# The second unit of differential attention ends ten groups of products later, and its results get rooms of their own

## The chip, the cores and the metric

One NeuronCore of a Trainium2 chip runs the whole program. The metric is device time in microseconds (us), the median of several runs. Engines are named as the profile names them: PE (matrix products), PEld (its weight loads), DVE (vector), ACT (activation), POOL (GpSimd), SP (which starts the DMAs here).

## The reference, cut to what matters

Two layers act on x (512 tokens x 1024, float32). Each normalises x, projects it, runs three branches side by side, gates each, and projects the sum back:

```
h = rms_norm(x, norm_g) * (1 + scale(c)) + shift(c);  proj = h @ w_in       # 3712 columns
A: 4 heads, two softmax maps each:  oa = rms_norm((softmax(q1 k1) - lam*softmax(q2 k2)) @ v) * (1 - lam_init) * silu(ga)
B: 6 heads, dilated windows (masked softmax over 512 keys):                    ob = attention(q, k, v) * silu(gb)
C: 4 heads of retention with a state carried over chunks:                      oc = rms_norm(retention) * silu(gc)
x = x + gate(c) * (concat(oa, ob, oc) @ w_out)
```

## The kernel before, in words

All large products run as three products of split operands: an operand is a high part and a rest (`whi`, `wlo` for weights, `hT`, `hL` for the activations), and `products` (L337) adds high x high, high x rest and rest x high in one PSUM bank, the tile `acc`, of which there are four. Such a set for two row blocks of the weights is a *group* of six products. The program is a list of numbered groups; `at(g, fn)` (L164) hangs a step behind group g, and `issue` walks through the list. In the first layer, groups 16 to 31 project the first unit of branch A (two of its heads; `Unit`, `Diff`), 32 to 47 the first of B, 48 to 63 the second unit of A, 64 to 79 and 80 to 95 the second and third of B, 96 to 111 the gate of branch C (its four token tiles take the four `acc` banks), 112 to 123 the gate of branch B (three blocks, three banks, lines L342 to L344), 124 to 155 the output projection. The second layer has the same order 172 groups further on. A unit's attention runs behind the projections of the units after it.

The list gives priorities, not the order of the queues: a planner in the framework places every instruction on its engine by costs and due times of its own, and hands a tile a room of its pool when one is free. So a step whose room is still held is placed later, and others go by.

The end of a unit of A is four steps. `finish` (L755) copies the attention's result from PSUM into `oat` (ACT). `finish2` (L760) turns it by four transposes on PE (`tr4`, one PSUM bank), copies that into `oao` (ACT), squares it (`oasq`, POOL), sums, and takes the power -1/2 (DVE, POOL). `finish3` scales `oao` (DVE) and multiplies by the gate `ga` (POOL). `finish4` turns it back and splits it into the two output tiles `o` that the output projection reads from group 132 on.

`oat`, `oao` and `oasq` lie in the pool `ep`, tag "e", of five rooms. In the same five lie the scores of A (`e`) and of B (`sb`, two to a row of 128 queries, from the mask step L807 until they are transposed), and `cth`, the gate of branch C: `gate_done` (L987, groups 108 to 111) computes tanh of an `acc` bank into `cth`, and a DVE step of L159 then reads the bank for the last time.

The score products use two PSUM banks (`sc`). The conditioning's gate uses them as well: `ada_steps` ends in a product into `ada_ps` (L479) and a copy into `gate` (ACT), which for the second half lies in the room of the second A unit's `ga`, and so waits for `finish3`.

For the second unit of A, `finish` is planned at 102 (48 + 54), `finish2` at 106, `finish3` at 118, `finish4` at 122:

```
            at(g + FIN2, self.finish2, g + FIN2)      # FIN2, FIN3, FIN4 = 4, 12, 16
            at(g + FIN3, self.finish3)
            at(g + FIN4, self.finish4)
```

Of the kernel before, what the change touches and what calls it, by code (L numbers as in the profile page):

```python
# [9 lines left out]
F32 = mybir.dt.float32  # L10
# [7 lines left out]
S = 512  # L18
L = 2
P = 128  # L20
# [3 lines left out]
DK_A, DV_A = 32, 64  # L24
# [22 lines left out]
SETUP, TABLES, RET_T, TAB1 = 12, 12, 19, 9        # L47
N_A1, N_B1, N_SOFT = 5, 5, 9
E_T1, E_T2, E_X, E_QF, E_SCALE_A, E_SCALE_B = 1, 1, 1, 0, 0, 0
FIN2, FIN3, FIN4 = 4, 12, 16  # L50
X_BACK = 2


# [81 lines left out]
def encoder(ctx, tc, x, c, norm_g, w_ada, b_ada, w_in, w_out, params, consts, out):  # L135
    nc = tc.nc
    pool = lambda name, bufs, **kw: ctx.enter_context(tc.tile_pool(name=name, bufs=bufs, **kw))
    one = pool("one", 1)
# [5 lines left out]
    ep = pool("ep", 5)  # L144
# [10 lines left out]
    def act(o, i, f=AF.Copy, **kw):  # L155
        A.activation(o, i, f, **kw)  # L156

    def stt(o, a, s, b, op0, op1):
        V.scalar_tensor_tensor(o, a, s, b, op0, op1)  # L159
# [4 lines left out]
    def at(g, fn, *args):  # L164
        plan.setdefault(g, []).append((fn, args))
# [118 lines left out]
    class Piece:  # L284


        def __init__(self, src, n, where=None, gains=(None, None)):
            self.src, self.n, self.where, self.gains = src, n, where, gains
# [5 lines left out]
        def split(self):  # L294
            if self.where:
                parts = self.where()
            else:
                parts = [[wp.tile([P, 2, 512], F32R, name=z)] for z in ("whi", "wlo")]
            self.hi, self.lo = ([z[:, k, :self.n] for z in y for k in range(z.shape[1])] for y in parts)
            k = 0  # L300
            for hi, lo in zip(*parts):
                m = hi.shape[1]
                r2, h2, l2 = self.raw[:, k:k + m, :self.n], hi[:, :, :self.n], lo[:, :, :self.n]
                g2 = self.gains[k:k + m]
                if not any(g is not None for g in g2):
                    act(h2, r2)

                for z, g in enumerate(g2):
                    if g is not None:
                        act(h2[:, z], r2[:, z], AF.Copy, scale=g)  # L310
                    elif any(y is not None for y in g2):
                        act(h2[:, z], r2[:, z])
                for z, g in enumerate(g2):
                    if g is None:
                        V.tensor_tensor(l2[:, z], r2[:, z], h2[:, z].bitcast(F32), OP.subtract)  # L315
                    else:
                        stt(l2[:, z], r2[:, z], g, h2[:, z].bitcast(F32), OP.mult, OP.subtract)
                k += m
# [34 lines left out]
    def tok_(t):  # L353
        return slice(t * P, (t + 1) * P)
# [72 lines left out]
    def in_chunk(l, cols, done, first=False):  # L427

        n = sum(z for _, z in cols)
        wheres = [room("stk"), None, rows((one, "b0"), (one, "b1"), (one, "b2"), (three, "v")),  # L430
                  rows((three, "v"), (three, "v"), (two, "pt"), (two, "pt"))]
        pieces = [Piece(win_src(l, k0, cols), n, wheres[k0 // 2] if first else None) for k0 in range(0, KD, 2)]
        g0 = len(groups)
        ps = {}

        def group(i, t):
            def emit():
                if t not in ps:
                    ps[t] = acc_p.tile([P, 512], F32, name="acc")
                p = pieces[i]  # L440
                products(ps[t][:, :n], [(hT[:, 2 * i + k, tok_(t)], hL[:, 2 * i + k, tok_(t)]) for k in range(2)],
                         p.hi, p.lo, n, i == 0, i == 3)
            return emit

        order = [(i, t) for t in range(NT) for i in range(4)] if first else [(i, t) for i in range(4) for t in range(NT)]
        for j, (i, t) in enumerate(order):
            groups.append(group(i, t))
            if i == 3:
                at(g0 + j, lambda t=t: done(t, ps[t], g0))
        for i, p in enumerate(pieces):  # L450
            piece_plan(p, g0 + (i if first else 4 * i))
        return g0, pieces
# [42 lines left out]
    def mod_steps(l, q):  # L495
        return ada_steps(l, [(q * 256, 256), (D + q * 256, 256)], lambda ps: mod_use(q, ps, mod_gain(l, q)))
# [72 lines left out]
    def tr4(blocks):  # L569
        ps = tr_p.tile([P, 4, P], F32, name="tr")  # L570
        for i, b in enumerate(blocks):
            T.transpose(ps[:, i, :], b, ident)  # L572
        return ps
# [12 lines left out]
    def rms_end(s, n, width):  # L586
        V.tensor_scalar(s, s, 1.0 / width, EPS, OP.mult, OP.add)  # L587
        pow_half(s, s, n)
# [130 lines left out]
                                 start=k == 0, stop=k == NT - 1)  # L719

    class Diff(Attention):
        def __init__(self, unit, g0, gap, oh, ol):
            self.oh, self.ol = oh, ol
            self.m = {}
            super().__init__(unit, g0, gap)

# [26 lines left out]
                self.e[qt, h] = self.m[2 * h]  # L753

        def finish(self, g):  # L755
            self.ob = ep.tile([P, S], F32, name="oat", tag="e")
            act(self.ob, self.pv)
            at(g + FIN2, self.finish2, g + FIN2)

        def finish2(self, g):  # L760
            ps = tr4([self.ob[:, tok_(t)] for t in range(NT)])
            o = self.o = ep.tile([P, 8, DV_A], F32, name="oao", tag="e")
            act(o.rearrange("p g d -> p (g d)"), ps.rearrange("p t m -> p (t m)"))
            sq = ep.tile([P, 8, DV_A], F32, name="oasq", tag="e")
            G.tensor_tensor(sq, o, o, OP.mult)
            ss = self.ss = sm.tile([P, 8], F32, name="oass")
            r0 = self.r0 = sm.tile([P, 8], F32, name="oar0")
            V.reciprocal(r0.rearrange("p (t h) -> p t h", h=2), self.ssum[:, :, 0::2])
            V.tensor_reduce(ss, sq, AX.X, OP.add)
            V.tensor_tensor(ss, ss, r0, OP.mult)  # L770
            V.tensor_tensor(ss, ss, r0, OP.mult)
            rms_end(ss, 8, DV_A)
            at(g + FIN3, self.finish3)
            at(g + FIN4, self.finish4)

        def finish3(self):
            o, ss = self.o, self.ss
# [5 lines left out]
        def finish4(self):  # L783
            on = self.o.rearrange("p (t h) d -> p t (h d)", h=2)
            ps = tr4([on[:, t] for t in range(NT)])
            split(self.oh, self.ol, ps.rearrange("p t m -> p (t m)"))

    class Dilated(Attention):
        def __init__(self, unit, g0, gap, ob, sg, out):
# [212 lines left out]
    def layer(l):  # L1002
# [15 lines left out]
        def out_pair(k):  # L1018
            oAB[k] = [one.tile([P, S], F32R, name=f"o{k}{z}", tag=f"s{2 * k + z}") for z in range(2)]
            return oAB[k]  # L1020

        def start_a(u, un, g, gap):
            Diff(un, g, gap, *out_pair(u))

        def start_b(u, un, g, gap):

# [4 lines left out]
        for kind, u, where, start, gap in (("A", 0, "A", START_A0, GAP_A0), ("B", 0, "B", START_B0, GAP_B0), ("A", 1, "A", START_A1, GAP_A1),  # L1031
                                           ("B", 1, "B", START_B1, GAP_B1), ("B", 2, "A", START_B2, GAP_B2)):
            if kind == "A":
                un = Unit(l, DK_A, 0, where)
                g0, _ = in_chunk(l, [(u * P + j * 256, P) for j in range(4)], un.done)
            else:
                un = Unit(l, DH_B, 2, where)
                g0, _ = in_chunk(l, [(COL_QB + u * P + j * 384, P) for j in range(3)], un.done)
# [48 lines left out]
        def plan_ada(steps, g, gap, g_end=0):  # L1087
            loads, adds, end = steps
            for i in range(4):
                at(g + gap * i - 6, loads[i])  # L1090
                at(g + gap * i, adds[i])
            at(max(g + gap * 4, g_end), end)
            return g + gap * 4
# [21 lines left out]
        for hf in range(2):  # L1115
            cols = slice(hf * 512, hf * 512 + 512)
            ps = {}
# [58 lines left out]
            for j, t in turns:  # L1176
# [9 lines left out]
                g = len(groups) - 1  # L1186
# [9 lines left out]
        if not last:  # L1196
            g = g_gb - MODS
            for q in range(4):
                g = plan_ada(mod_steps(l + 1, q), g, 3)
# [116 lines left out]
```

## Time and profile before

| | us |
|---|---|
| median of 3 runs (649.25 to 651.51) | 651.46 |
| the profiled execution, its own time | 650.6 |
| its span, first to last instruction | 648.7 |

The profile is of one execution; a row of a timeline gives start, duration, engine, line, operation and tiles, and in brackets how long the engine stood idle before it and what ended that.

### The profile page before, as it was taken

The page shows a single profiled execution, that of the slowest core. Times are in us where ns is not written, and L with a number is a line of the kernel's source. Part 1 is how long each engine was busy: PE and PEld are TensorE (multiplying, and loading weights), DVE is VectorE, ACT ScalarE, POOL GpSimd, SP SyncE. Part 2 cuts the span into 40 slices and gives each one's busy share as a digit, 9 for nine tenths or more (in the row PEclk, how much of TensorE's full clock was granted, in tenths as well). Part 3 has the DMA queues.
Part 4 walks back from the last instruction along what each step waited for, and adds up shares of the span by engine and source line. Part 5 has one row for each costly group of instructions (what it writes and reads, how often), then busy time and mean ns, then how long its engine had stood idle before and what let it go on. Part 6 is the DMA issues. An engine that isn't in the chain of part 4 may idle for free.

```text
span 648.7 us, 10469 instructions
## 1 busy us (share of the span) xinstructions
PE 622.2 (96%) x3487; PEld 512.2 (79%) x3487; DVE 491.8 (76%) x1206; ACT 344.4 (53%) x756; POOL 163.7 (25%) x183
## 2 busy tenths in 40 slices
PE   6899999999999996999999999999999999899997
PEld 1788888987888873677779998997788787677786
DVE  4787676689988987898969364768997997578443
ACT  4855263566646665564424344455756577566410
POOL 1105452514350510200411041633323340020000
PEclk9799999999999999999999999999999999999999
DMA  8998123535555556476643322235565453604211
GB/s 302 295 293 238 55 70 98 135 98 146 150 152 176 141 176 161 160 248 201 216 156 110 90 73 66 71 104 159 134 176 137 135 145 112 161 34 149 80 65 66
DMA packets 87277, 93.03 MB, mean 143 GB/s; under 512 B 7188, under 2 KB 68276, under 8 KB 87224
## 3 DMA queue, kind: packets, MB, share of 16 engines
q1 hardware_dynamic: 87224, 92.37, 48.0%
q8 instruction: 28, 0.46, 0.3%
q14 instruction: 25, 0.20, 0.1%
HBM read 72.42 MB, written 4.19 MB: 118 GB/s over the span
## 4 chain that ended last, share of the span: by engine, by line
PE 79%; DVE 9%; issue 4%; DMA 3%; POOL 3%; ACT 2%; SPq 1%; POOLq 0%; ACTq 0%
PE acc L346 16%; PE acc L348 16%; PE acc L347 16%; PE tr L572 8%; PE pv L718 5%; PE sc L741 2%; DMA x<-in_x_dram 2%; PE acc L344 1%; PE acc L342 1%; PE acc L343 1%; PE sc L802 1%; PE sc L803 1%; DVE wlo L315 1%; PE co L971 1%; DVE pt L708 1%
## 5 line engine op out<-in xcount | busy, mean ns | idle before, releaser
L346 PE MATMUL acc<-whi,hT 128*128 128x384 f32 (+1 forms) x424 | 154.7, 365 | 0.0
L347 PE MATMUL acc<-wlo,hT 128*128 128x384 f32 (+1 forms) x424 | 151.8, 358 | 0.0
L348 PE MATMUL acc<-whi,hL 128*128 128x384 f32 (+1 forms) x424 | 151.8, 358 | 0.0
L315 DVE TENSOR_TENSOR wlo<-raw,whi 128x384 fp32r<-128x384 f32 (+1 forms) x130 | 80.7, 650 | 26.7 <-ACT whi L156 26.4
L199 POOL TENSOR_TENSOR qkss<-qkss,nhalf 128x4 f32<-128x4 f32 (+1 forms) x40 | 52.6, 1315 | 128.3 <-DVE qkss L587 127.3
L346 PEld LDWEIGHTS acc<-whi,hT 128*128 128x128 f32 x424 | 80.0, 189 | 6.1
L348 PEld LDWEIGHTS acc<-whi,hL 128*128 128x128 f32 x424 | 79.8, 188 | 6.2
L347 PEld LDWEIGHTS acc<-wlo,hT 128*128 128x128 f32 x424 | 80.0, 189 | 5.5
L156 ACT ACTIVATE whi<-raw 128x768 fp32r<-128x768 f32 (+2 forms) x67 | 59.5, 890 | 39.7 <-PE acc L348 33.8
L159 DVE SCALAR_TENSOR_TENSOR ada_acc<-raw,cs,ada_acc 128x512 f32<-128x512 f32 x86 | 64.3, 749 | 3.9 <-DMA raw<-in_w_ada_dram 3.3
L156 ACT ACTIVATE e<-sc,mx 128x512 f32<-128x512 f32 x64 | 43.9, 689 | 35.5 <-DVE mx L743 16.9
L743 DVE TENSOR_REDUCE mx<-sc 128x1 f32<-128x512 f32 x64 | 43.5, 685 | 9.5 <-PE sc L741 8.8
L156 ACT ACTIVATE sb<-sb,mx 128x512 f32<-128x512 f32 x48 | 34.4, 717 | 20.4 <-DVE mx L807 20.2
L718 PE MATMUL pv<-pt,v 128*64 128x256 f32 x320 | 38.9, 385 | 1.0 <-DVE pt L708 0.9
L156 ACT ACTIVATE pt<-tr 128x512 f32<-128x512 f32 x40 | 23.8, 596 | 23.1 <-PE tr L572 22.9
L572 PE MATMUL tr<-cst,sb 128*128 128x128 f32 x192 | 30.7, 283 | 5.3 <-DVE nat L159 2.2
L807 DVE CUSTOM_DVE_ANT_0 sb<-sc,cst 128x512 f32<-128x512 f32 x48 | 32.1, 683 | 4.4 <-PE sc L803 2.6
L572 PEld LDWEIGHTS tr<-cst,sb 128*128 128x128 f32 x192 | 21.9, 142 | 16.0 <-ACT pt L156 7.7
L718 PEld LDWEIGHTS pv<-pt,v 128*64 128x64 f32 x320 | 21.2, 136 | 16.2 <-DVE pt L708 5.5
L708 DVE COPY pt<-tr 128x512 f32<-128x512 f32 x40 | 27.4, 684 | 7.8 <-PE tr L572 7.8
L639 POOL TENSOR_TENSOR qkn<-qkraw,qkss 128x256 f32<-128x256 f32 x40 | 30.0, 751 | 5.9 <-DVE qkraw L635 2.0
L741 PE MATMUL sc<-stk,stq 96*128 96x512 f32 x64 | 27.3, 434 | 1.0 <-ACT e L156 0.9
(294 smaller groups left out, 1367.8 us busy)
## 6 DMA issues: line engine op xcount, KB each, us to landing
raw<-in_w_ada_dram SPq DMA_DIRECT2D x64, 256.0 KB, 3.2
raw<-in_w_in_dram SPq DMA_DIRECT2D x48, 192.0 KB, 2.9
raw<-in_w_in_dram SPq DMA_DIRECT2D x24, 384.0 KB, 3.4
raw<-in_w_in_dram SPq DMA_DIRECT2D x32, 256.0 KB, 3.4
raw<-in_w_ada_dram SPq DMA_DIRECT2D x16, 512.0 KB, 5.1
raw<-in_w_out_dram SPq DMA_DIRECT2D x32, 256.0 KB, 3.0
x<-in_x_dram SPq DMA_DIRECT2D x8, 512.0 KB, 4.2
stB<-nat SPq DMA_DIRECT2D x32, 128.0 KB, 2.4
```

The lines of the kernel that those rows point to most:

```text
L156: A.activation(o, i, f, **kw)
L159: V.scalar_tensor_tensor(o, a, s, b, op0, op1)
L199: G.tensor_tensor(o, i, nhalf[:, :n], OP.pow)
L315: V.tensor_tensor(l2[:, z], r2[:, z], h2[:, z].bitcast(F32), OP.subtract)
L346: T.matmul(ps, ah, hi[i], start=s_, stop=False)
L347: T.matmul(ps, ah, lo[i], start=False, stop=False)
L348: T.matmul(ps, al, hi[i], start=False, stop=e_)
L572: T.transpose(ps[:, i, :], b, ident)
L708: V.tensor_copy(pt, ps)
L718: T.matmul(self.pv[h * 64:h * 64 + 64, i * 256:i * 256 + 256], self.u.v[:, k, h * 64:h * 64 + 64], self.pt[h][:, k], start=k == 0, stop=k ...
L741: T.matmul(ps, self.u.stq[0:96, m, tok_(qt)], self.u.stk[0:96, m], start=True, stop=True)
L743: V.tensor_reduce(mx, ps, AX.X, OP.max, negate=True)
```

## The change

The second unit of A gets offsets of its own: `finish2` 14 groups behind `finish` (not 4), `finish3` 6 and `finish4` 9 behind that, so 116, 122 and 125 (not 106, 118, 122). The first unit keeps 4, 12, 16. For both units `oat` and `oao` leave the pool "e": they lie in the pool `one`, in the rooms of the unit's output pair (tags s0 and s1, or s2 and s3), and the pair itself is taken in `finish4`, when `oat` and `oao` are through, rather than at the unit's start. `oasq` stays in "e". No computation is added or left out.

```diff
-FIN2, FIN3, FIN4 = 4, 12, 16
+FIN_A = (4, 12, 16), (14, 6, 9)
-        def __init__(self, unit, g0, gap, oh, ol):
-            self.oh, self.ol = oh, ol
+        def __init__(self, unit, g0, gap, fin, k, out_pair):
+            self.k, self.out_pair, self.fin = k, out_pair, fin
         def finish(self, g):
-            self.ob = ep.tile([P, S], F32, name="oat", tag="e")
+            self.ob = one.tile([P, S], F32, name="oat", tag=f"s{2 * self.k + 1}")
             act(self.ob, self.pv)
-            at(g + FIN2, self.finish2, g + FIN2)
+            at(g + self.fin[0], self.finish2, g + self.fin[0])
         def finish2(self, g):
             ps = tr4([self.ob[:, tok_(t)] for t in range(NT)])
-            o = self.o = ep.tile([P, 8, DV_A], F32, name="oao", tag="e")
+            o = self.o = one.tile([P, 8, DV_A], F32, name="oao", tag=f"s{2 * self.k}")
...
-            at(g + FIN3, self.finish3)
-            at(g + FIN4, self.finish4)
+            at(g + self.fin[1], self.finish3)
+            at(g + self.fin[2], self.finish4)
         def finish4(self):
...
-            split(self.oh, self.ol, ps.rearrange("p t m -> p (t m)"))
+            split(*self.out_pair(self.k), ps.rearrange("p t m -> p (t m)"))
         def start_a(u, un, g, gap):
-            Diff(un, g, gap, *out_pair(u))
+            Diff(un, g, gap, FIN_A[u], u, out_pair)
```

## Rows read from the trace of the kernel before

**Rows 1.** The page: busy time of the engines; PE's busy tenths in 40 slices.
```profile
PE 622.2 (96%) x3487; PEld 512.2 (79%) x3487; DVE 491.8 (76%) x1206; ACT 344.4 (53%) x756; POOL 163.7 (25%) x183
...
PE   6899999999999996999999999999999999899997
```

**Rows 2.** Windows: from:to us, length, busy by engine, then PEclk, DMA share, GB/s.
```profile
232.00:272.00 40.00, 33.81 (x190) 23.98 (x188) 34.54 (x83) 22.76 (x49) 5.29 (x5) 0.96 0.57 162
...
260.00:262.00 2.00, 2.00 (x8) 1.41 (x8) 1.75 (x6) 0.88 (x2) 0.00 (x0) 0.50 0.86 259
```

**Rows 3.** Timeline of PE, first layer, end of branch C's gate products.
```profile
241.07 0.39 PE L802 MATMUL sc<-stB,stC 128*128 128x512 f32 x1
...
241.52 0.34 PE L347 MATMUL acc<-wlo,hT 128*128 128x384 f32 x1
...
243.44 0.60 PE L572 MATMUL tr<-cst,sb 128*128 128x128 f32 x4
243.79 0.42 PE L346 MATMUL acc<-whi,hT 128*128 128x384 f32 x1
...
244.22 0.33 PE L348 MATMUL acc<-whi,hL 128*128 128x384 f32 x1
...
251.04 0.66 PE L572 MATMUL tr<-cst,sb 128*128 128x128 f32 x4 [0.69 <-ACT pt L156]
...
257.22 0.66 PE L572 MATMUL tr<-cst,oat 128*128 128x128 f32 x4 [0.78 <-DVE pt L708]
...
259.54 0.79 PE L342 MATMUL acc<-hT,whi 128*128 128x512 f32 x1
```

**Rows 4.** Windows by line (L572 twice, L802 twice, L718): PE busy (count), PEld.
```profile
244.30:259.50 15.20, 5.37 (x32) 3.37 (x32) 0.98 0.69 169
558.70:567.60 8.90, 3.28 (x20) 2.09 (x20) 1.00 0.81 198
...
244.30:259.50 15.20, 1.94 (x4) 0.76 (x4) 0.98 0.69 169
558.70:567.60 8.90, 0.95 (x2) 0.38 (x2) 1.00 0.81 198
...
244.30:259.50 15.20, 1.95 (x16) 1.06 (x16) 0.98 0.69 169
```

**Rows 5.** Timeline of ACT and DVE, first layer, around the same stretch.
```profile
239.93 0.59 ACT L156 ACTIVATE oat<-pv 128x512 f32<-128x512 f32 x1
...
244.07 0.69 DVE L807 CUSTOM_DVE_ANT_0 sb<-sc,cst 128x512 f32<-128x512 f32 x1
...
244.59 0.85 ACT L156 ACTIVATE whi<-raw 128x768 fp32r<-128x768 f32 x1
...
257.92 0.60 ACT L156 ACTIVATE oao<-tr 128x512 f32<-128x512 f32 x1 [2.19 <-PE tr L572]
258.41 0.49 ACT L156 ACTIVATE cth<-acc 128x384 f32<-128x384 f32 x1
```

**Rows 6.** Timeline of PE and ACT, second layer, the same place.
```profile
559.23 0.66 PE L572 MATMUL tr<-cst,sb 128*128 128x128 f32 x4 [0.33 <-ACT pt L156]
...
567.64 0.50 PE L342 MATMUL acc<-hT,whi 128*128 128x512 f32 x1 [0.31 <-DVE cth L159]
...
566.52 0.49 ACT L156 ACTIVATE cth<-acc 128x384 f32<-128x384 f32 x1
```

**Rows 7.** Timeline, first layer: second half of the conditioning's gate; POOL and DVE.
```profile
232.62 1.02 PE L479 MATMUL ada_ps<-ada_acc,ones 128*128 128x512 f32 x2
...
271.49 0.60 ACT L156 ACTIVATE gate<-ada_ps 128x512 f32<-128x512 f32 x1 [1.50 <-POOL oao L781]
...
272.14 0.50 PE L802 MATMUL sc<-stk,stq 128*128 128x512 f32 x1 [0.63 <-ACT gate L156]
...
258.59 1.04 POOL L765 TENSOR_TENSOR oasq<-oao 128x512 f32<-128x512 f32 x1 [24.36 <-ACT oao L156]
...
270.46 1.88 DVE L315 TENSOR_TENSOR wlo<-raw,whi 128x384 fp32r<-128x384 f32 x2
```

## The prediction

> **What bounds the kernel now.** I read the page first: PE is busy 96% of the span, DVE 76%, so the kernel is bound by PE wherever PE has work [rows 1]. A gain must therefore come from places where PE stands, and a cost must make it stand. PE's slices show where: between the first two and the last, all 37 are 9s but for the 6 at place 16 and the 8 at place 35 [rows 1]. A slice is 648.7 / 40 = 16.2 us, so they are 243 to 259 and 551 to 568, one in each layer. The windows put numbers to the first: in 232 to 272 PE is busy 33.81 of 40 us and its granted clock averages 0.96; in 260 to 262 the clock is 0.50, that is the lower level of 1.2 GHz, and what came before it was PE with holes in its work [rows 2].
>
> The timeline of PE then shows what is missing. The last product of C's gate starts at 244.22, and the first of B's gate at 259.54 [rows 3]; in the second layer the first of B's gate waits until 567.64 [rows 6]. In between PE does only attention. Weights are not what lacks: the last ones that could be split had their copy at 244.59 [rows 5]. What lacks is a PSUM bank. All four `acc` hold C's gate until `gate_done` has read them, and its first `cth` starts on ACT at 258.41, directly behind `oao` at 257.92 [rows 5], which follows the turn of `oat` at 257.22 [rows 3]. 1.13 us later the first product of B's gate starts. So `cth` waits for a room of the five of "e", and the room it gets is `oat`'s, held since 239.93 [rows 5]. That the rooms are full is seen on the other holders: an `sb` starts at 244.07 [rows 5], 0.03 us after the set of turns of an older `sb` from 243.44 ends [rows 3]. Two rows of `sb` are four rooms, `oat` is the fifth.
>
> The second layer repeats it: `cth` at 566.52, first product 1.12 us later at 567.64 [rows 6].
>
> **How much lies open.** In 244.30 to 259.50 PE has 32 transposes (8 sets), 4 score pairs and one set of 16 value products [rows 4]. At full rate a set costs 0.35 (243.44 to the product at 243.79) and a pair 0.45 (241.07 to 241.52) [rows 3]; the values took 1.95 [rows 4]. 8 x 0.35 + 4 x 0.45 + 1.95 = 6.55, so of 15.2 us 8.65 are open. In the second layer 5 sets, 2 pairs and one set of values in 8.9 us [rows 4]: 4.60, open 4.30. The low clock cost (1 - 0.96) x 40 = 1.6 us more in the first layer [rows 2].
>
> **The change, part by part.**
>
> *`oat` and `oao` out of "e", and `finish2` ten groups later.* Each request for a room then gets the release before the one it got. The last `sb` of B's second unit takes what the set before 251.04 releases, and the first `cth` what the set at 251.04 releases, at 251.04 + 0.66 = 251.70, not what `oat` leaves. `oao` and `oasq`, which asked ahead of `cth`, now ask behind it. With the same 1.13 us from `cth` to product, B's gate starts at 252.83 and not 259.54: 6.71 us to fill. In these the other work of PE is at most the values (1.95), three sets (1.05) and one pair (0.45), 3.45; `oat`'s set goes, but comes back as 0.35 in a full stretch. Regained: 6.71 - 3.45 - 0.35 = 2.9, and the clock's 1.6 if it doesn't fall: 4.5. In the second layer the set at 559.23 [rows 6] releases at 559.89, the first product is at 561.01 and not 567.64; 6.63 - 3.45 - 0.35 = 2.8. Together 7.3.
>
> The bounds. If `cth` gets a room as soon as its bank is summed, nothing is open: 8.65 + 1.6 + 4.30 - 0.70 = 13.9. If nothing moves, -0.7. DVE is a bound of its own in the first layer: busy 34.54 of 40 [rows 2], it has 5.5 us to give there unless work is put off, so I stay near the row with 4.5.
>
> *The steps moved.* `finish2` has four transposes (PE), one copy (ACT), the square and the power (POOL), a reciprocal, a sum and three small steps (DVE); none starts a DMA, so SP's queue is only touched through rooms. On POOL they pass a memset of `ada_acc`. They now lie beside B's gate, where PE has products to run; the turns I counted.
>
> The square is one price to weigh: 1.04 us, begun at 258.59 after 24 us of an idle POOL [rows 7], while DVE had little to do; moved, it runs beside a full DVE. By the Trainium skill (SBUF — State Buffer, "Who interferes with whom") a DVE instruction with two SBUF inputs is blocked for the whole of a POOL instruction that reads SBUF. The trace agrees as far as it goes: beside the POOL multiplication that ended ahead of 271.49, two `wlo` steps of 384 columns took 1.88 [rows 7], where a step of 512 columns takes 0.69 [rows 5]. By that rule DVE would lose up to 1.04 us a layer, and the gain would be up to 2.1 us less if DVE decided. I leave the sum as it is, for the bound by DVE leaves 1 us.
>
> *The second half of the conditioning's gate.* It adds no wait, but lengthens one. `ada_ps` holds one of two score banks from 232.62 until the copy at 271.49, which stood 1.50 us for POOL's multiplication by `ga` in `finish3`; PE then stood 0.63 us for the copy [rows 7]. `finish3` moves from 118 to 122. Behind the copy on ACT are the exponentials of B's third unit, and PE's score product waits for it. Below: the earlier start of B's gate makes up for the four groups, cost nothing. Above: every score row of the third unit (four a layer) runs on one bank and its second head waits for the first's mask step, 0.69 [rows 5], and its own half pair, 0.22: 0.9 x 8 = 7.2. Four groups are 24 products of half a pair, 24 x 0.225 = 5.4 us; the start is 6.7 earlier. So I take the value near the row: one such wait in each layer, where there is one in the first now: +0.6.
>
> *`finish4` at 125, not 122.* Its results are read from 132 on: seven groups, 42 products x 0.225 = 9.5 us, for a set of turns, a copy and a subtraction. Cost nothing; with that cover gone, PE would stand for these, some 0.7 us each.
>
> *The rooms s0 to s3.* Their earlier tenants, C's values, are read last at the end of C's chunks, long before 70 and 102; `finish4`'s pair takes rooms that its own turns have just released. Nothing.
>
> *The first unit.* Its `oao` held a room of "e" for 16 groups while the second unit needed four to a row. There PE's slices are 9s throughout [rows 1]; bounds 0 to -1.5 (a tenth of a slice), I take 0.
>
> Sum: 7.3 - 0.6 = 6.7. The profiled execution took 650.6 (span 648.7 and 1.9 around it): 643.9. The median is 0.86 above it, so 651.46 - 6.7 = 644.8.
>
> **Rivals.**
>
> *The gap closes wholly.* The room freed is there from 239.93 on, and C's banks are summed at 244; a `cth` that is ready then may be given it at once. For it: weights for B's gate are ready. Against: the `sb` of B's second unit are ahead in the list and ask too, and DVE's 5.5 us. 651.46 - 13.9 + 0.6 = 638.2, and with part of it 641.
>
> *The room goes elsewhere, or DVE was the limit.* The planner hands rooms by its own times; with `sb` taking every early room and DVE full, as it is until about 253, the third and fourth rows come no sooner, and `cth` still follows the last turns. Then PE gains what it loses: 648.5 to 653, say 651. Against it: two of three holders ahead of `cth` are gone.
>
> *The score bank, on the other side: slower.* If B's gate starts only a little earlier (half of the gain, 3.3) and `ga` is read late, behind the second score row of B's third unit, all eight rows pay: 651.46 - 3.3 + 7.2 = 655.4. It decides from the point where the copy into `gate` ends later than that second row. For it: 39 us of hold already [rows 7], and `finish3` later in the list. Against: while one score waits, PE has up to nine groups of B's gate to run, and a planner that fills with those pays little.
>
> **How the numbers follow.** Forecast (641 to 648.5) 0.55; closed wholly 0.15; no change 0.18; score bank 0.12. What this measurement can tell is about 0.5%, 3.3 us. All of the first two cases lie below 648.2 but for a sliver, so faster 0.70; same 0.18; slower 0.12. The range that leaves out about the bank's 0.12 above, some of the upper end of no change and the tail under the second case is 638.5 to 652; the forecast's own is 641 to 648.5.
>
> **What would show it.** Right: the first L342 product near 253 and 561 less what was gained before, in front of the turn of `oat`; no 6 and no 8 among PE's 9s; no 0.50 in the clock there; `cth` first on ACT without `oao` ahead of it. The score bank would show as PE's waits for the copy into `gate` or for a mask step of B's third unit, well over 0.63. If the first L342 product is still more than 12 us behind C's last, the room was not the cause; if it is early and the time stays, look where PE stands next, at DVE's late `wlo` and B's third unit.

## The result, and the profile after

The changed kernel takes 644.04 us (median of 4 runs, 643.31 to 644.49) beside 650.88 us for the kernel before: a ratio of 0.9897, 95% interval 0.9876 to 0.9918. The forecast was 644.8. The profiled execution took 644.29 us, its span 642.2.

The page after, the lines that answer to [rows 1], with the clock's line: engines, PE's busy tenths, PE's granted clock in tenths.

```profile
PE 620.4 (97%) x3487; PEld 512.2 (80%) x3487; DVE 492.3 (77%) x1206; ACT 343.1 (53%) x756; POOL 163.9 (26%) x183
...
PE   6899999999999997999999999999999999999997
...
PEclk9799999999999997999999999999999999999999
```

The 8 at place 35 has gone, the 6 at place 16 is only a 7, and the clock has a 7 at place 16, which it did not have before. The window of [rows 2] again, after the change:

```profile
232.00:272.00 40.00, 36.37 (x200) 26.79 (x199) 36.50 (x86) 23.86 (x51) 0.69 (x2) 0.91 0.68 197
250.00:252.00 2.00, 2.00 (x12) 1.18 (x10) 2.00 (x4) 0.49 (x1) 0.00 (x0) 0.50 0.90 204
```

PE is busy 2.56 us more of the 40, but the mean clock is 0.91, so the low clock costs up to (1 - 0.91) x 40 = 3.6 us, 2 more than before. PE's timeline of the first layer shows where it fell (compare [rows 3]); the stretch between the last product of C's gate and the first of B's is called the seam below:

```profile
241.95 0.42 PE L348 MATMUL acc<-whi,hL 128*128 128x384 f32 x1
...
246.31 0.63 PE L572 MATMUL tr<-cst,sb 128*128 128x128 f32 x4 [1.94 <-DVE nat L159]
247.63 0.71 PE L572 MATMUL tr<-cst,sb 128*128 128x128 f32 x4 [0.69 <-ACT pt L156]
249.12 3.68 PE L718 MATMUL pv<-pt,v 128*64 128x256 f32 x16 [0.78 <-DVE pt L708]
...
254.50 0.59 PE L342 MATMUL acc<-hT,whi 128*128 128x512 f32 x1
```

and ACT's, where `cth` no longer follows `oao` [rows 5]:

```profile
248.46 0.47 ACT L156 ACTIVATE cth<-acc 128x384 f32<-128x384 f32 x1
...
274.56 0.60 ACT L156 ACTIVATE oao<-tr 128x512 f32<-128x512 f32 x1 [1.77 <-PE tr L572]
...
285.10 0.60 ACT L156 ACTIVATE gate<-ada_ps 128x512 f32<-128x512 f32 x1 [2.32 <-POOL oao L782]
```

`cth` starts 0.12 us after the set of turns of 247.63 ends: by its time it got the room that this set released, as the prediction had it. A bank was free from about 249.6, but PE had the values, a set and a score pair in front of the first product, and its clock had fallen: the 16 value products took 3.68 us, not 1.95 [rows 4].

In the second layer (compare [rows 6]) nothing is left open: PE's two rows are the last product of C's gate and the first of B's.

```profile
558.72 0.33 PE L348 MATMUL acc<-whi,hL 128*128 128x384 f32 x1
558.89 0.40 PE L342 MATMUL acc<-hT,whi 128*128 128x512 f32 x1
```

Where the time went is best read as a lead: how much sooner than before the same product or turn starts in PE's timeline. Below: the first product with `whi`, at 64.99 before and ahead of every step that an edit moves ("start"); the first product into `ada_ps`, at 229.34 before and ahead of the seam ("229 us"); the first product of B's gate and of the output projection in the first layer, the first turn of the next layer's activations, the first product of the output projection in the second layer, the last product.

| us sooner than before | start | 229 us | B's gate, layer 1 | projection, layer 1 | next layer's turns | projection, layer 2 | last product |
|---|---|---|---|---|---|---|---|
| the change | 0.52 | 3.14 | 5.04 | 5.13 | 3.23 | 7.08 | 6.55 |
| e1 rooms only | 0.80 | 3.39 | 1.33 | 2.44 | 2.43 | 3.83 | 3.82 |
| e2 delay only | 1.37 | 1.29 | 2.88 | 3.90 | 2.34 | 4.12 | 3.61 |
| e3 second unit alone | 1.23 | 1.15 | 4.37 | 5.02 | 4.30 | 6.38 | 5.85 |
| e11 rooms, square out | 0.32 | 2.73 | 4.41 | 3.98 | 3.97 | 7.23 | 7.21 |
| e6 gate's room | 0.97 | 3.54 | 4.55 | 5.22 | 4.76 | 7.60 | 7.15 |
| e8 before, `cth` out | -0.59 | -0.65 | 13.39 | 10.68 | 7.71 | 10.50 | 10.49 |
| e9 change, `cth` out | 1.58 | 4.17 | 15.98 | 15.99 | 9.38 | 11.42 | 10.91 |
| e10 e9 and gate's room | -0.16 | 2.43 | 16.78 | 15.03 | 11.50 | 14.56 | 14.12 |
| e12 before, both | 0.72 | 0.68 | 13.11 | 12.70 | 8.67 | 10.28 | 10.20 |
| e13 e10, no delay | 0.23 | 2.83 | 17.18 | 15.25 | 11.83 | 15.67 | 15.68 |

Each line is one execution, and the executions differ by some 2 us before anything that was edited has run; so a lead is read from its own start. Read so, the change gives 2.7 us in the first layer (3.23 - 0.52) and 3.3 in the second.

Two readings follow. The first: 2.4 to 2.6 us are there at 229 us, before the seam, in every kernel that has the first unit's `oat` and `oao` outside "e", and none in e2, e3, e8 and e12, which leave them there. Two waits of PE in the kernel before are gone in the former and stand in the latter:

```profile
195.08 0.50 PE L802 MATMUL sc<-stB,stC 128*128 128x512 f32 x1 [1.07 <-ACT e L156]
...
210.52 0.49 PE L741 MATMUL sc<-stk,stq 96*128 96x512 f32 x1 [0.87 <-ACT e L156]
```

The second: of the 1.9 us by which the lead falls between the projection and the next layer's turns, PE stood 1.04 (0.58 at 289.13 and 0.46 at 291.64, for two `pt`), where it had no wait before. Another 0.35 is no loss: the set of turns of `oao` now lies behind the projection's first product instead of ahead of it. The last 0.5 no row names. In e8, where values and turns of B's third unit lie behind it too, the lead falls by 3.0 without any wait.

### The profile page after: what moved, and what is told of

Read it like the earlier page. It is cut to its first block, busy times and chain, and to the rows that moved or that the text cites. A ratio compares the mean times of both kernels' runs of the same rounds, so it can differ in the third digit from the quotient of the medians.

```text
span 642.2 us, 10455 instructions
## 1 busy us (share of the span) xinstructions
PE 620.4 (97%) x3487; PEld 512.2 (80%) x3487; DVE 492.3 (77%) x1206; ACT 343.1 (53%) x756; POOL 163.9 (26%) x183
## 4 chain that ended last, share of the span: by engine, by line
PE 82%; DVE 7%; issue 4%; DMA 3%; POOL 3%; ACT 1%; SPq 1%; POOLq 0%; ACTq 0%
PE acc L346 17%; PE acc L348 17%; PE acc L347 17%; PE tr L572 8%; PE pv L718 5%; PE sc L741 2%; DMA x<-in_x_dram 2%; PE sc L803 1%; PE acc L342 1%; PE acc L344 1%; PE acc L343 1%; PE sc L804 1%; PE co L972 1%; PE kv L939 1%; PE co L971 1%
## 5 line engine op out<-in xcount | busy, mean ns | idle before, releaser
L315 DVE TENSOR_TENSOR wlo<-raw,whi 128x384 fp32r<-128x384 f32 (+1 forms) x130 | 79.4, 634 | 25.6 <-ACT whi L156 25.5
L199 POOL TENSOR_TENSOR qkss<-qkss,nhalf 128x4 f32<-128x4 f32 (+1 forms) x40 | 54.2, 1354 | 124.9 <-DVE qkss L587 123.8
L718 PE MATMUL pv<-pt,v 128*64 128x256 f32 x320 | 40.7, 398 | 1.4 <-DVE pt L708 1.2
L718 PEld LDWEIGHTS pv<-pt,v 128*64 128x64 f32 x320 | 21.8, 141 | 16.8 <-DVE pt L708 5.2
L572 PE MATMUL tr<-cst,sb 128*128 128x128 f32 x192 | 30.4, 280 | 3.2 <-DVE nat L159 1.9
L572 PEld LDWEIGHTS tr<-cst,sb 128*128 128x128 f32 x192 | 22.2, 142 | 13.1 <-ACT pt L156 5.6
```

Source lines behind the costliest of these rows:

```text
L199: G.tensor_tensor(o, i, nhalf[:, :n], OP.pow)
L718: T.matmul(self.pv[h * 64:h * 64 + 64, i * 256:i * 256 + 256], self.u.v[:, k, h * 64:h * 64 + 64], self.pt[h][:, k], start=k == 0, stop=k ...
```

## The experiments

**e1, rooms without the delay.** The changed kernel with

```diff
-FIN_A = (4, 12, 16), (14, 6, 9)
+FIN_A = (4, 12, 16), (4, 12, 16)
```

> Changed kernel with its second unit's steps back at 4, 12 and 16 groups; oat and oao keep rooms of their own. Theory of the room (the gain is that cth no longer waits for the room that oat held): most of the gain stays, cth first runs near 249 in the first layer although the turn of oat is early, the gate of the conditioning is copied early again (near 271, not 285), so no late wait on the score bank: 643 to 646 us. Rival of the delay (the gain is that the turns and copies of finish2 are out of the way of B's second unit): the gain is gone, 650 to 651 us.

Measured: 648.2 us, ratio 0.9969 (0.9951 to 0.9987), between the two theories. Its ten runs spread from 647.02 to 651.01, and the profiled one is the lowest. PE and ACT, first layer:

```profile
247.38 0.83 PE L572 MATMUL tr<-cst,sb 128*128 128x128 f32 x4 [0.69 <-ACT pt L156]
...
258.21 0.50 PE L342 MATMUL acc<-hT,whi 128*128 128x512 f32 x1 [0.32 <-DVE cth L159]
```
```profile
256.58 0.60 ACT L156 ACTIVATE oao<-tr 128x512 f32<-128x512 f32 x1 [2.23 <-PE tr L572]
257.08 0.87 ACT L156 ACTIVATE cth<-acc 128x384 f32<-128x384 f32 x2
```

A room came free at 248.2, as in the changed kernel, yet `cth` is again behind `oao`. Either the square's tile `oasq`, ahead of it in the list, had the claim on that room, or `cth` was merely queued behind `oao` on ACT: e11 tells these apart. In the first layer the seam gave nothing here: of the 3.39 us of lead at 229 us, 1.33 are left at B's gate. What this layer gains is the first unit's.

**e2, the delay without rooms.** The kernel before with the new offsets for its second unit, `oat` and `oao` in "e".

```diff
-            at(g + FIN2, self.finish2, g + FIN2)
+            at(g + self.fin[0], self.finish2, g + self.fin[0])
...
```

> Kernel before with the second unit's steps at 14, 6 and 9 groups; oat and oao stay in the five rooms of e. Theory of the room: oat holds its room all the longer, only oao and oasq no longer ask ahead of cth, so cth moves by one or two releases at most (first product of B's gate near 256 in the first layer, not 254.5) and the gate is late as well: 648 to 652 us. Rival of the delay: 644 to 645 us.

Measured: 647.92 us, 0.9951 (0.9936 to 0.9966), so again half, against the rival. `cth` starts half a microsecond behind the first set of turns that follows the values; before, it came behind the third:

```profile
254.35 0.66 PE L572 MATMUL tr<-cst,sb 128*128 128x128 f32 x4
...
256.66 0.50 PE L342 MATMUL acc<-hT,whi 128*128 128x512 f32 x1 [0.32 <-DVE cth L159]
```
```profile
255.53 0.49 ACT L156 ACTIVATE cth<-acc 128x384 f32<-128x384 f32 x1
```

The halves, 0.31% and 0.49%, add up to 0.80% beside the 1.03% of both, a difference that the intervals do not show. By the account so far each leaves a claim ahead of `cth`, e1 the square's and e2 the room that `oat` holds.

**e3, the second unit alone.** The changed kernel, the first unit's `oat` and `oao` back in "e".

```diff
-            self.ob = one.tile([P, S], F32, name="oat", tag=f"s{2 * self.k + 1}")
+            self.ob = one.tile(...) if self.k else ep.tile([P, S], F32, name="oat", tag="e")
...
```

> Changed kernel, but the first unit's oat and oao stay in e; the second unit has own rooms and the delay. If the first unit's rooms are worth nothing, as predicted: 644 us. Rival of the first unit (the last product of C's gate is 2.3 us earlier in the first layer after the change, which the room held for 16 groups by the first unit's oao would explain): 646 to 648 us, and that last product is back near 244.

Measured: 644.93 us, 0.9907 (0.9892 to 0.9921), not to be told from the change's 0.9897. By the time the first unit's rooms are worth nothing that shows. In the trace they do show: without them PE waits again for `e` (1.06 us at 193.87, 0.87 at 209.32), there is no lead at 229 us, and the last product of C's gate is back at 245.10, as the rival had it. But the seam then gives more. At the next layer's turns this kernel is 3.1 us ahead of its own start, and the change 2.7: what the first unit's rooms gave had been spent at the seam.

**e8, `cth` out of the five rooms, and nothing of the change.** The direct test.

```diff
-            th = ep.tile([P, 384], F32, name="cth", tag="e")
+            th = one.tile([P, 384], F32, name="cth", tag=f"s{8 + t % 2}")
```

> Kernel before, nothing of the change; only the four cth of branch C's gate lie in two rooms of their own (tags s8 and s9, idle then) instead of the five of e. Theory of the room: cth runs as soon as its bank is summed, the first product of B's gate follows the last of C's gate at once in both layers (near 245 and 560), PE keeps its clock, and 8 to 10 us are gained: 641 to 643 us. Rival (the delay, or DVE is what holds the stretch): not below 647 us.

Measured: 638.57 us, 0.9809 (0.9794 to 0.9824), nearly twice the gain of the change, and more than the 641 to 643 us that were expected. PE's rows at the seam, and the window of [rows 2]:

```profile
244.86 0.34 PE L348 MATMUL acc<-whi,hL 128*128 128x384 f32 x1
...
246.15 0.39 PE L342 MATMUL acc<-hT,whi 128*128 128x512 f32 x1
```
```profile
232.00:272.00 40.00, 39.84 (x231) 30.38 (x230) 38.06 (x95) 26.07 (x55) 4.17 (x4) 1.00 0.66 189
```

The first product of B's gate follows 1.3 us behind the last of C's; PE is full and its clock doesn't fall. So the room is what held the stretch, and DVE, which was busy for 38.06 of 40 us where it had been for 34.54, did not. In the second layer the first product of B's gate follows 0.6 us behind C's last (550.99).

**e11, the square out as well.** e1 with

```diff
-            sq = ep.tile([P, 8, DV_A], F32, name="oasq", tag="e")
+            sq = one.tile([P, 8, DV_A], F32, name="oasq", tag="s8")
```

> Changed kernel with the second unit's steps back at 4, 12 and 16, and oasq, the last of that unit's tiles in e, in a room of its own (s8). With rooms alone, cth came at 257.1 in the first layer, behind oao on ACT. If it was oasq's claim on a room ahead of cth that held it: cth first near 249, the first product of B's gate near 254, and 644 us or better with the gate copied early. If it was its place behind oao in ACT's queue: cth again directly behind oao near 257, and 647 to 648.5 us as with rooms alone.

Measured: 642.56 us, 0.9867 (0.9842 to 0.9892), where e1 had 0.9969. ACT, first layer:

```profile
249.06 0.49 ACT L156 ACTIVATE cth<-acc 128x384 f32<-128x384 f32 x1
...
258.07 0.60 ACT L156 ACTIVATE oao<-tr 128x512 f32<-128x512 f32 x1 [2.51 <-PE tr L572]
```

`cth` is ahead of `oao` and near 249, so its place in ACT's queue was not what held it in e1. What is left of the two is the claim: `oasq`, planned at 106, had the room from 248 on, some nine us before the square could run, and `cth`, planned at 108, had to take the next ones. With no claim ahead of it, the steps need not be late at all.

**e6, the score bank.** The changed kernel, and

```diff
-                z[hf] = two.tile([P, 512], F32, name="gate", tag="ga")
+                z[hf] = two.tile([P, 512], F32, name="gate", tag=("pt", "ga")[hf])
```

> Changed kernel; the first half of the conditioning's gate lies in a room of another tag (pt of the pool two), so the second half takes the room of the first unit's ga and no longer waits for finish3 of the second unit. Theory of the score bank (after the change PE's lead in the first layer falls from 5.1 us at the end of B's gate to 3.2 at the layer's end because the score bank is held until the gate's copy at 285): the copy comes early, the lead stays near 5, and 642 us or a little less. Rival (that loss is DVE's, from POOL's steps beside it and from work put off): 644 us, the lead still falls by about 2.

Measured: 643.37 us, 0.9878 (0.9854 to 0.9901): by the time not to be told from the change. In the first layer the trace does what the theory says: the second half's copy comes at 232.03, not 285.10, and the lead of 5.2 falls only to 4.8 by the next layer's turns, not to 3.2, without the two waits of 1.04. But e3, whose copy is as late as the change's (283.31), has no such wait there either, so the copy's lateness alone does not make them. In the second layer PE stands 1.85 us for DVE's `pt` at 580.99, where the longest wait of the change is 0.52, and the gain is gone.

```profile
232.03 0.57 ACT L156 ACTIVATE gate<-ada_ps 128x512 f32<-128x512 f32 x1
```

**e9 and e10, the change with `cth` out, without and with the gate's room** (the edits of e8 and e6).

> Changed kernel, and the four cth in two rooms of their own (s8, s9) as in the kernel before with cth out, which took 638.6 us. If the change does nothing but give cth its room, there is nothing left for it: 638 to 639 us, with the late copy of the gate perhaps 1 to 2 us on top (640). Rival (the delay helps by itself, by keeping finish2's turns out of B's second unit): 635 to 637 us.

> As the one with the change and cth out, and also the gate's rooms as in the first kernel of this set. If the late copy of the gate costs 1 to 2 us there, this takes them back: 637 to 638.5 us. Rival (PE is full by then and the bank costs nothing): the same as without it, within 0.2%.

Measured: e9 639.75 us, 0.9824 (0.9796 to 0.9853); e10 635.96 us, 0.9764 (0.9739 to 0.9789). Here the bank does show: the two intervals are apart, if only just. In e9 PE stood for the copy, three times as long as in [rows 7]:

```profile
282.93 0.50 PE L803 MATMUL sc<-stk,stq 128*128 128x512 f32 x1 [1.85 <-ACT gate L156]
```

The late copy is the price of the delay, and once `cth` has its own room the delay buys nothing: e9 is no faster than e8, which has none of the change.

**e12 and e13, both edits on the kernel before, and on the change without its delay.** e13 is e10 with the line of e1.

> Kernel before with the four cth in s8 and s9 and the first half of the conditioning's gate in the tag pt; nothing of the change. With the change these two edits took 0.9764 of the time before. If rooms and the score bank were all there was, this is as fast: 0.975 to 0.979, 635 to 638 us. Rival (the change keeps something of its own: its delay, or the rooms of e that it frees): 0.980 or more, no better than with cth out alone (0.9809).

> The fastest so far (change, cth out, gate's room) with the second unit's steps back at 4, 12 and 16 groups. If the delay is worth nothing once no room is short: 0.975 to 0.978. Rival of the delay: slower by 1 to 2 us, 0.979 to 0.980, with PE waiting in B's second unit for ACT's oao or the turns' bank.

Measured: e12 640.31 us, 0.9841 (0.9818 to 0.9864); e13 635.02 us, 0.9748 (0.9734 to 0.9761), the fastest of all. e13 beside e10 says that the delay is worth nothing when no room is short. e12 beside e13 says that `oat` and `oao` out of "e" are still worth 0.9% with `cth` out. In the traces e13's lead, read from its start, is 6.0 us larger than e12's at the last product, and 2.6 of these are there at 229 us, by the first unit's rooms, which here are not spent again. Where the rest comes from no run separates. e12 isn't faster than e8, though the bank is free in it. Read from its start, its lead is 0.7 us larger than e8's at the projection of the first layer and 1.6 smaller at the last product; in its second layer PE stands 2.02 us at 564.08 for DVE's `pt`, and DVE itself had stood 1.75 for POOL's power of `finish2` (`oass`). e8's longest wait there is 0.49. Why the steps meet so in one and not in the other stays open.

## Why the prediction was right

*The place and the cause* held: the first L342 products came sooner and `cth` has left `oao`'s shadow. By its time the room it took was that of the set that was named. e8 and e11 show that a claim on a room held it, and e8 that DVE did not.

*One sign of being wrong* came up, and misled: "more than 12 us behind C's last, the room was not the cause". The first product is 12.55 us behind C's last (254.50, 241.95), and the room was the cause all the same (e8). The first unit's rooms had brought C's last product forward, so the distance no longer measured what was gained.

*The first layer* had 4.5 us for the seam. Read from its start it gave 4.6 by the projection and 2.7 by the next layer's turns, and not from the terms of the sum: 2.6 were there before the seam. The first product came at 254.50, not 252.83, though `cth` came 3.2 us earlier than the 251.70 reckoned; each row of B's second unit had its room earlier too. The clock's 1.6 did not come back: the fall came earlier, with the values inside it, and cost up to 3.6. The step that failed there is "and the clock's 1.6 if it doesn't fall". The mean clock of 232 to 272 is 0.91 in the change, e1, e6 and e11, which have the first unit's rooms; it is 0.96 in the kernel before, e2 and e3, which don't. The length of the seam does not sort them: it is 16.5 us in e1 and 10.1 in e3.

*The second layer* had 2.8; the lead grows there from 3.2 to 7.1 at the projection, 3.9, for its gap closed wholly.

*The first unit's* 0 holds for the time (e3) and not for PE. "PE's slices are 9s throughout" was read from slices of 16.2 us, which show a 9 with the waits of 1.07 and 0.87 in them. Without them PE is 2.6 us ahead at 229 us; at the seam that was lost again in the change, and with `cth` out it was kept (e13 beside e12).

*The score bank* had +0.6 in all: one wait a layer, where the first had one already (0.63). Its lower bound was that "the earlier start of B's gate makes up for the four groups". It did not: the copy moved from 271.49 to 285.10, for `finish2` was behind 49 of the 72 products of B's gate, and then the chain had to be run through against a full DVE. In the first layer PE stood 1.79 us between the first product of B's gate and the next layer's turns (0.75 for a mask step of B's third unit, and the two `pt`), against 0.63 before and 0.68 with the gate's room (e6). That is 1.2 more where the sum had nothing more: mis-sized, and on the side of the rival that bore its name, whose 7.2 in full was never near. It is not the bank's alone, since e3 stood 0.72 with the late copy. In the second layer PE stood 0.52 for a mask step, close to the 0.6. The 0.5 of lead that goes behind the projection there goes without any wait, in e6 too: the turns of `oao` lie behind it.

*POOL's square* was left out of the sum. Moved beside a full DVE, it and the multiplication were longer, and one DVE step was caught in each layer; in the first:

```profile
275.24 1.51 POOL L766 TENSOR_TENSOR oasq<-oao 128x512 f32<-128x512 f32 x1 [11.06 <-ACT oao L156]
...
283.27 1.80 POOL L782 TENSOR_TENSOR oao<-oao,ga 128x512 f32<-128x512 f32 x1 [1.55 <-DVE bs L814]
```
```profile
283.83 1.52 DVE L819 TENSOR_SCALAR sb<-sb,bs 128x512 f32<-128x512 f32 x1
```

The square took 1.04 before and the multiplication 1.28 (at 270.17). The DVE step has a median of 0.48 over its 24 executions; it took 1.52 here and 1.43 in the second layer (at 585.37), and ends both times 0.28 after POOL's. By the Trainium skill (SBUF — State Buffer, "Who interferes with whom") a DVE `tensor_scalar` can contend with a GpSimd instruction for the ports that both use, and the one that issues first has them for its whole length while the other is blocked. The trace agrees, with 1.04 and 0.95 us for DVE. What of it PE felt no run here separates. e3 and e6, with the same delay, have multiplications of 1.28 and 1.29 in the first layer and not the two waits for `pt`.

*The rivals*: "closes wholly" was what e8 did, by another edit; below the 638 to 641 that were given for it came only e10 and e13, which have the change's rooms and the gate's room besides. "The room goes elsewhere" is what happened in e1, by the square's claim; DVE as the limit fell in e8.

*Luck.* The total fits better than its parts. The sum said 6.7 us, the medians say 6.8 and the traces, read from their starts, 6.0. But the layers gave 2.7 for 4.5 and 3.3 for 2.2 (2.8 less the bank's 0.6), and in the first the 2.6 of the first unit, which the sum had at 0, stood against the clock, whose 1.6 it had counted as regained.

## What to carry to other kernels

When PE stands without products, ask which bank they need, who must read that bank first, and where that reader's own output is to lie: here a stall of PE was two steps away from the shortage of an SBUF room. Tiles that are planned early and written late claim rooms from those that could run, so a rotating pool should hold only tiles that are written as soon as a room is free. Give the reader that frees a shared bank a room of its own (0.9809, one line) before moving the holders out of its way (0.9897), and look for what else is released by the steps you delay. Read a lead at a point ahead of the stretch that you changed as well, and look for waits inside slices that are marked full: 2.6 of the 5.1 us at the projection were there before the seam, where two waits of about 1 us had gone.

## What the runs showed of the hardware

The granted clock fell to its lower level (0.50) in the changed kernel between 248 and 250, after a stretch in which PE still ran turns and score products between its waits; the 16 value products took 3.68 us there and 1.95 at the upper level, so a hole is paid for a second time by what runs behind it. In e8, without the hole, the same window has a mean clock of 1.00.
